# Where the squares of the first token half are taken for the MLP norm: in the tails, or where the mixers make that half

## The chip, the cores and the metric

The kernel runs on one core of a Trainium2 chip. The metric is the device time of one execution in microseconds. Engines are named as in the profile: PE does matrix products, DVE, ACT and POOL work on vectors, SP issues most of the DMAs.

## What is computed

The reference is a trunk of two layers over 1024 tokens of width 1024. Layer 0 mixes with two groups of recurrent heads, layer 1 with chunked attention. Each layer adds a mixer and then an MLP to the residual, and then a gated embedding:

```python
x = x + mix                                    # mix = heads' output @ w_out
hf = rmsnorm(x, norm_ffn_g[i])                 # x * rsqrt(mean(x*x) + eps) * g
x = x + jnp.square(jax.nn.relu(hf @ mlp_w1[i])) @ mlp_w2[i]
x = x + rmsnorm(p[i] @ ple_w_proj[i], ple_norm_g[i]) * jax.nn.sigmoid(x @ ple_w_gate[i])
```

The change is about `mean(x*x)` in the second line: one sum of 1024 squares for each token.

## The kernel before

Data stand with the 1024 features on 8 tiles of 128 partitions (n = 0..7) and the tokens along the free dimension. The tokens are worked on in two halves of 512 (`hs[0]`, `hs[1]`). Products are in float32 split into a high and a low part, so that one product of 128x128 by 128x512 is three matmuls (`mm3`): high with high, low with high, high with low. A "dense" is one output tile for one half: 8 such triples, 24 matmuls into one PSUM bank.

`trunk` runs, for each layer, the mixer with its lanes (`layer0_in`, `layer1_in`) and then `tail(i)`.

The mixer's last lane is `out_early` (L1798). It waits for the heads' results of the first half, and for n = 0..7 makes the output projection of that half as one dense; its `ev` adds the residual on DVE (L1829) and sends the sum x to DRAM as `xh[n]` (L1830, on SP). Then it makes the first part of the second half's projection (`part`): those matmuls need heads of the second half, of which the last come late in layer 0, since its recurrence runs through all tokens.

The tail begins with the second half's projection and with the norm's input. For each n:

- `load_x` (L1320, L1321) fetches the residual's second half (from `in_x` in layer 0, from `xd` in layer 1) and `xh[n]` into the buffer `xr[n % 2]`.
- `first_half` (L1339, L1340) splits the first half, scaled by the norm's weight, into high and low parts on ACT and DVE; `scaled` (L1324, ACT) keeps a scaled copy; `square(n, 0)` adds its squares to `accs[0]`.
- `ev_out` (from L1354) does the same for the second half when its dense is done: DVE adds, SP sends `xm[n]`, `scaled`, and `square(n, 1)` adds to `accs[1]`. Differences of quarters for the MLP's products (`combine` L1348, splits L1304 and L1308) come in between.
- `square` (L1331, L1334, L1335) is a Square on ACT into one of two `sq` buffers and an add into the accumulator on POOL; for n = 0 the Square goes straight into the accumulator.

The MLP multiplies blocks of weights (not of activations) by activations that aren't normalised yet; the norm's factor is put on its results. Each of its block products is cut into seven products of sums of quarters, m = 1..7 in `order`. After the fifth of them (q == 4) `row_sums` (L360) multiplies 4 + 4 pieces of the two accumulators by a column of ones on PE (`ones,acc`); after the sixth, `row_norms` scales the sums on DVE (`ms`, L374) and takes the inverse square root in 13 small steps on POOL (L274 to L279, result `col`). `to_rows` (L377) then turns `col` into rows with 8 transposes on PE (`ident,col`, L178) and two ACT copies into `rs` (L385), with which POOL scales the first results (`late<-late,rs`).

The order on each engine: the program is scheduled when it is built, by a scheduler with a model of its own, which orders an engine's instructions freely as far as their dependences allow. In the tail's MLP the products and the vector steps are pinned to the written order; the transposes of `to_rows` are not. Buffers are pools of tagged tiles: `act` gives out tiles of a pool with 6 places for the tag "a". Two PSUM banks serve the mixer's denses, 6 more the tail's.

In layer 1, `out_early` reads the residual's first half into tiles of four n (`xt`), and `acc` is the tile in which `ple_proj`, which ran ahead of it, summed squares of its own; it is free after that.

Of the kernel before, what the change touches and what calls it, by code (L numbers as in the profile page):

```python
# [8 lines left out]
F32 = mybir.dt.float32  # L9
F32R = mybir.dt.float32r  # L10
I32 = mybir.dt.int32
AF = mybir.ActivationFunctionType
ALU = mybir.AluOpType
# [4 lines left out]
P = 128  # L18
T = 1024
D = 1024  # L20
NK = D // P
HB = 512
NT = T // P
# [92 lines left out]
class Trunk:  # L116
# [252 lines left out]
    def row_norms(self, ps, out, scale=1.0 / D, eps=1e-6, pool=False):  # L369

        nc = self.nc
        nt = out.shape[-1]
        ms = self.sm.tile([P, NT], F32, tag="ms", name="ms")[:, 0:nt]
        nc.vector.tensor_scalar(ms, ps[:, 0:nt], scale, eps, op0=ALU.mult, op1=ALU.add)  # L374
        self.rsqrt_small(out, ms, [P, nt], "n", pool)

    def to_rows(self, col, out):  # L377

        nc = self.nc
        for hf in range(col.shape[-1] // 4):  # L380
            pb = self.stat_bank()
            for j in range(4):
                i = hf * 4 + j
                self.tr(pb[:, j * P:(j + 1) * P], col[:, i:i + 1].broadcast_to((P, P)), self.ident)
            nc.scalar.copy(out[:, hf * HB:(hf + 1) * HB], pb)  # L385
# [174 lines left out]
    def l0_in(self, units):  # L560
        nc, a, fr = self.nc, self.a, self.fr
        self.state = {}
        self.xg = []
        for u, (nm, p, hf) in enumerate(units):
            if u % 8 == 0:
# [3 lines left out]
                if hf == 0:  # L569
                    acc = fr.tile([P, HB], F32, tag="rsbc", name="acc", bufs=2)  # L570
# [75 lines left out]
        rsb = lambda: fr.tile([P, HB], F32, tag="rsbc", name="xs", bufs=2)  # L646
# [1 line left out]
        sc = [self.pair(q, F32) for q in (2, 3)]  # L648
        sc = [t[:, e] for t in sc for e in range(2)]
        yield from self.ple_proj(0, lambda k, hf: pt[k][:, hf], sc[0], lambda n: sc[1 + n % 3], rsb, self.load_w)  # L650
        yield from self.out_early(0, a["x"], self.pair, rsb, self.load_w, [("post", 7), ("post", 13), ("post", 14), ("post", 15)])

    def load_x(self, q, pool, tag):

# [579 lines left out]
    def tail(self, i, xsrc):  # L1234
# [9 lines left out]
        nc, tc, a = self.nc, self.tc, self.a  # L1244
# [3 lines left out]
        with ExitStack() as es:  # L1248
# [43 lines left out]
            accs = [self.accp.tile([P, HB], F32, tag=f"acc{hf}", name="acc") for hf in range(2)]  # L1292
            col = self.cst.tile([P, NT], F32, tag="col", name="col")
# [29 lines left out]
            def scaled(n, hf):  # L1323
                A.activation(xs[:, n % 2, hs[hf]], xr[n % 2][:, hs[hf]], AF.Copy, scale=self.vec("ffng", 8 * i + n))  # L1324
            b11, b12, b21, b22 = quarters(xs)

            def square(n, hf):

                t = xr[n % 2][:, hs[hf]]
                if n == 0:  # L1330
                    A.activation(accs[hf], t, AF.Square)  # L1331
                else:
                    sq = sqs()
                    A.activation(sq, t, AF.Square)  # L1334
                    G.tensor_tensor(accs[hf], accs[hf], sq, op=ALU.add)  # L1335

            def first_half(n):
                c, t, g = cmb[1 + n % 2][n // 2], xr[n % 2][:, hs[0]], self.vec("ffng", 8 * i + n)
                A.activation(c[:, 0], t, AF.Copy, scale=g)  # L1339
                V.scalar_tensor_tensor(c[:, 1], t, g, c[:, 0].bitcast(F32), op0=ALU.mult, op1=ALU.subtract)  # L1340
                scaled(n, 0)
                square(n, 0)

            def combine(m, j):
                if m == 3:
# [125 lines left out]
            def at(slot, f, *args):  # L1471
                jobs.setdefault(slot, []).append((f, *args))
# [99 lines left out]
            for q, m in enumerate(order):  # L1572
                for f, *args in ahead[q]:
                    f(*args)
                part_0[m] = product(0, m, range(4 if q < 2 else 3))
                if q < 2:
                    at(q + 2, ev_1, 0, q, m, part_0[m])
                do(q)
                if q == 4:
                    stats = self.row_sums(accs, col)  # L1580
                elif q == 5:
                    self.row_norms(stats, col, pool=True)
                yield 0
            for q, m in enumerate(order[2:]):
                for f, *args in ahead[q + 7]:
# [24 lines left out]
            x = tiles_x(F32)  # L1610
# [184 lines left out]
                nc.sync.dma_start(out=self.pnd[n], in_=t)  # L1795
        self.row_stats([acc[:, 0, :], acc[:, 1, :]], self.prsc)

    def out_early(self, i, xsrc, pair, xt, load_w, keys):  # L1798

        nc, a = self.nc, self.a  # L1800
        self.xh = [self.dr.tile([P, HB], F32, tag=f"xh{k}", name="xh") for k in range(NK)]
        pairs = [(0, 1), (2, 4), (5, 6), (3, 7)] if i == 0 else [(0, 1), (2, 3), (4, 5), (6, 7)]
        self.order = [k for pr in pairs for k in pr]

        def load(q, hf):
            raw = self.wr.tile([P, 2, HB], F32, tag="wraw", name="yr")
            t = pair(q)
            for e, k in enumerate(pairs[q]):
                y[k] = t[:, e]
                if (k, hf) == (7, 1):  # L1810
                    self.ylast = y[k]
                else:
                    nc.sync.dma_start(out=raw[:, e], in_=self.yd[k][hf])
                    self.split_scaled(y[k], raw[:, e], None, slice(0, HB))
        y, self.wod = {}, {}
        yield keys[0]
        for q in range(4):
            load(q, 0)
        for n in range(NK):
            w = load_w(a[f"w_out{i}"][n])  # L1820
            if n > 2 - i:
                self.wod[n] = self.dr.tile([P, 2, T], F32, tag=f"wod{n}", name="wod")
                for e in range(2):
                    nc.sync.dma_start(out=self.wod[n][:, e], in_=w[e].bitcast(F32))
            x = xt()
            nc.sync.dma_start(out=x, in_=xsrc[n][:, 0:HB])

            def ev(ps):
                nc.vector.tensor_tensor(x, x, ps, op=ALU.add)  # L1829
                nc.sync.dma_start(out=self.xh[n], in_=x)  # L1830
            yield from self.dense_part(w, y, ev, self.order)
        y = {}
        yield keys[1]
        ws = []
        for q in range(3):
            load(q, 1)
            if q < 2:
                ws.append(load_w(a[f"w_out{i}"][q]))
        if i == 0:
            raw = self.wr.tile([P, T], F32, tag="wraw", name="wraw")  # L1840
            nc.sync.dma_start(out=raw, in_=a["w_out0"][2])
            self.w_next = self.split_w(raw, T, [self.pre.tile([P, T], F32R, tag=f"p{q}", name="w" + q) for q in "hl"])
        self.first = [self.bank() for _ in ws]

        def part(ks):
            for (hi, lo), ps in zip(ws, self.first):
                for k in ks:
                    o = slice(k * P, k * P + P)
                    self.mm3(ps, hi[:, o], lo[:, o], y[k][:, 0, :], y[k][:, 1, :], k == 0, k == 7)
                    yield 0  # L1850
        yield from part(self.order[:6])
        yield keys[2]
        load(3, 1)
        self.mark(("ylast", 0))
        yield from part(self.order[6:7])
        yield keys[3]
        yield from part([7])
        self.y = y
# [21 lines left out]
    def attn_ins(self, steps, l1):  # L1880
        kv = {}
        for s, (pr, hf) in enumerate(steps):
            if s >= 3:
                yield ("at", s - 3)
            self.st[s] = yield from self.attn_in(pr, hf, l1, kv)
            self.mark(("qk", s), self.lat["qk"])

        act = self.act
        ws = {}

        def load_w(src):
            n = ws["n"] = ws.get("n", -1) + 1
            if n % 3 == 0:
                ws["h"], ws["l"] = self.weights3(n // 3 % 2)
            raw = self.wr.tile([P, T], F32, tag="wraw", name="wraw")
            self.nc.sync.dma_start(out=raw, in_=src)
            hi, lo = ws["h"][:, n % 3, :], ws["l"][:, n % 3, :]
            self.nc.scalar.copy(hi, raw)
            self.nc.vector.tensor_tensor(lo, raw, hi.bitcast(F32), op=ALU.subtract)
            return hi, lo  # L1900
        p = [act([P, 2, T], F32R, "b") for _ in range(2)]
        acc = act([P, 2, HB], F32)
        t = [act([P, 2, 2, HB], F32) for _ in range(4)]
        yield from self.ple_proj(1, lambda k, hf: p[k][:, :, hf * HB:hf * HB + HB], acc, lambda n: t[n // 2][:, n % 2],
                                 lambda: self.wp.tile([P, HB], F32, tag="sq", name="sq", bufs=1), load_w)
        q = {}

        def xt():
            n = q["n"] = q.get("n", -1) + 1
            if n % 4 == 0:  # L1910
                q["x"] = act([P, 4, HB], F32)
            return q["x"][:, n % 4, :]
        yield from self.out_early(1, self.xd, lambda q: act([P, 2, 2, HB], F32R), xt, load_w,
                                  [("at", 14), ("at", 14), ("at", 14), ("at", 15)])

    def attn_norms(self, steps, l1):
        K = []
# [311 lines left out]
```

## Time and profile before

| | us |
|---|---|
| median of 3 executions (lowest, highest) | 3065.73 (3061.58, 3071.53) |
| the profiled execution, on the device clock | 3063.73 |
| its span from the first to the last instruction | 3062.0 |

The mean granted clock of PE over the span is 0.975 of full speed. The stretches that the change touches, in time on the profile's clock:

| stretch | what runs there |
|---|---|
| 819 to 879 | layer 0: the 8 denses of `out_early` beside the recurrence |
| 879 to 917 | layer 0: first parts of the second half, and the recurrence's last steps |
| 917 to 957 | layer 0's tail: second half of the projection, first halves read back |
| 957 to 987 | layer 0: MLP products 1 to 7, the norm's sums and factor |
| 2247 to 2290 | layer 1: the 8 denses of `out_early` |
| 2290 to 2335 | layer 1's tail: second half of the projection |
| 2335 to 2366 | layer 1: MLP products 1 to 7, the norm's sums and factor |

A row of a timeline gives start, duration, engine, line, operation, `out<-in`, shapes, how many instructions the row joins, and in brackets how long the engine stood before it and who let it go. A row of windows gives for a stretch its length, then for each engine the busy time and the number of instructions, then PE's granted clock, the mean busy share of the DMA engines, and GB/s.

### The profile page before, as it was taken

To read this page: it belongs to the slowest core of one execution; us is meant where nothing else is said; L and a number is where in the kernel's file an instruction comes from. 1 tells how busy PE (TensorE), PEld (TensorE's weight loads), DVE (VectorE), ACT (ScalarE), POOL (GpSimd) and SP (SyncE) were. 2 spreads that over 40 slices of the span, in tenths; PEclk is the share of its full clock that TensorE was granted. 3 is DMA by queue.
4 is the path that set the end of the run, shared out by engine and by line. 5 is a ranking of instruction groups with operands and counts; after the bars stand their busy time and mean duration, and the time that the engine had idled before them with its cause. 6 is when DMAs were issued, how large, how long until landed. Compare 5 with 4: busy or idle time off the path is not lost. (4 is left out here: it accounts for less than half of the span.)

```text
span 3062.0 us, 45242 instructions
## 1 busy us (share of the span) xinstructions
PE 2958.2 (97%) x16888; PEld 2488.1 (81%) x16888; DVE 2217.9 (72%) x3680; ACT 1409.4 (46%) x2546; POOL 1255.6 (41%) x1396
## 2 busy tenths in 40 slices
PE   8999999998989999999999999999999999999999
PEld 6888778877877888788888899998887888788887
DVE  6756765667748888877676687877858888877672
ACT  4444443434435544543333466656645544543331
POOL 5535533444504666645445100000204666645442
PEclk9999989998999999999999999999999999999999
DMA  3231212212444434655323211110275444654322
GB/s 129 95 96 56 74 45 77 75 60 76 154 158 177 155 151 151 237 203 176 123 91 122 71 45 41 41 57 17 78 283 188 155 152 151 232 207 176 123 94 100
DMA packets 166765, 374.31 MB, mean 122 GB/s; under 512 B 41360, under 2 KB 45584, under 8 KB 165136
## 3 DMA queue, kind: packets, MB, share of 16 engines
q1 hardware_dynamic: 134288, 312.68, 29.6%
q10 hardware_dynamic: 32256, 58.73, 5.1%
q8 instruction: 133, 2.18, 0.3%
q14 instruction: 88, 0.72, 0.1%
HBM read 259.15 MB, written 112.20 MB: 121 GB/s over the span
## 5 line engine op out<-in xcount | busy, mean ns | idle before, releaser
L173 PE MATMUL dps<-r,act 128*128 128x512 f32 x4440 | 1043.0, 394 | 9.6 <-DVE act L113 8.3
L173 PEld LDWEIGHTS dps<-r,act 128*128 128x128 f32 x4440 | 836.2, 189 | 199.9 <-DVE act L113 16.1
L173 PE MATMUL dps<-xg,whi 128*128 128x512 f32 x1248 | 421.4, 416 | 14.6 <-ACT xg L342 7.1
L113 ACT CAST act<-late 128x512 fp32r<-128x512 f32 (+1 forms) x282 | 205.5, 731 | 445.4 <-DVE late L113 263.2
L113 DVE TENSOR_TENSOR act<-late,act 128x512 fp32r<-128x512 f32 (+1 forms) x282 | 330.9, 1175 | 71.7 <-ACT act L113 68.4
L173 PE MATMUL dps<-wq,act 128*128 128x384 f32 x1536 | 302.8, 345 | 6.9 <-DVE vs L1987 2.5
L173 PEld LDWEIGHTS dps<-xg,whi 128*128 128x128 f32 x1248 | 237.9, 196 | 65.1 <-ACT xg L342 7.1
L173 PEld LDWEIGHTS dps<-wq,act 128*128 128x128 f32 x1536 | 264.3, 190 | 12.2 <-DVE vs L1987 4.1
L173 PE MATMUL dps<-xg,wlo 128*128 128x512 f32 x624 | 257.3, 413 | 0.8 <-DVE wlo L299 0.8
L113 POOL TENSOR_TENSOR late<-late 128x512 f32<-128x512 f32 (+1 forms) x104 | 186.5, 1802 | 78.6 <-ACT late L113 57.0
L113 POOL TENSOR_TENSOR late<-late,rs 128x512 f32<-128x512 f32 x88 | 137.5, 1575 | 102.1 <-DVE late L113 94.1
L1994 POOL TENSOR_TENSOR sq<-qk 128x512 f32<-128x512 f32 x32 | 35.7, 1116 | 312.4 <-ACT qk L1982 286.9
L113 DVE TENSOR_TENSOR r<-act,r 128x1024 fp32r<-128x1024 f32 (+1 forms) x80 | 140.3, 1755 | 6.7 <-ACT r L113 6.7
L173 PEld LDWEIGHTS dps<-xg,wlo 128*128 128x128 f32 x624 | 121.7, 195 | 26.5 <-DVE wlo L299 1.2
L113 DVE TENSOR_TENSOR late<-late 128x512 f32<-128x512 f32 x120 | 142.3, 1186 | 1.0
L173 PE MATMUL dps<-xw,act 128*128 128x512 f32 x576 | 139.1, 394 | 3.1 <-ACT act L113 3.1
L173 PEld LDWEIGHTS dps<-xw,act 128*128 128x128 f32 x576 | 108.5, 189 | 27.8 <-ACT act L113 3.5
L2082 ACT ACTIVATE pb<-pb,mx 128x640 f32<-128x640 f32 (+4 forms) x128 | 89.5, 699 | 85.5 <-DVE mx L2080 83.1
L299 DVE TENSOR_TENSOR wlo<-wraw,whi 128x1024 fp32r<-128x1024 f32 x76 | 96.0, 1264 | 36.6 <-ACT whi L298 35.6
L298 ACT CAST whi<-wraw 128x1024 fp32r<-128x1024 f32 x76 | 79.5, 1048 | 89.5 <-PE dps L173 56.7
L113 DVE TENSOR_TENSOR late<-late,dps 128x512 f32<-128x512 f32 x154 | 104.7, 682 | 19.7 <-ACT late L113 15.5
L113 ACT ACTIVATE late<-late 128x512 f32<-128x512 f32 x176 | 110.6, 631 | 13.4 <-POOL late L113 9.8
(504 smaller groups left out, 5823.6 us busy)
## 6 DMA issues: line engine op xcount, KB each, us to landing
late<-in_w SPq DMA_DIRECT2D x100, 512.0 KB
hc<-late ACTq DMA_DIRECT2D x154, 256.0 KB
act<-hc SPq DMA_DIRECT2D x76, 512.0 KB
wraw<-in_w_in SPq DMA_DIRECT2D x56, 512.0 KB
hraw<-hc SPq DMA_DIRECT2D x36, 512.0 KB
hc<-sums ACTq DMA_DIRECT2D x70, 256.0 KB
act<-in_w SPq DMA_DIRECT2D x28, 512.0 KB
wraw<-in_w_out SPq DMA_DIRECT2D x21, 512.0 KB
```

Source lines behind the costliest of these rows:

```text
L113: return lambda *args, **kw: self.tc.keep_in_program_order(f(*args, **kw))
L173: r = self.nc.tensor.matmul(out, lhsT, rhs, start=start, stop=stop)
L298: nc.scalar.copy(hi, raw)
L299: nc.vector.tensor_tensor(lo, raw, hi.bitcast(F32), op=ALU.subtract)
L1994: G.tensor_tensor(sq, q4[:, 8 * e:8 * e + 8], q4[:, 8 * e:8 * e + 8], op=ALU.mult)
L2082: A.activation(S, S, AF.Exp, bias=mx[:, 1:2], accum_out=l)
```

## The change

`square(n, 0)` leaves the tail's `first_half`. In its place `out_early` takes the squares of each x of the first half while it is still on chip: an ACT Square and a POOL add for each n (for n = 0 the Square alone, into the accumulator). Behind the eighth dense it makes the 4 sums of that half on PE and scales them on DVE into columns 0 to 3 of a new tile `mlp_ms`. The tail makes only the second half's 4 sums, scales them into columns 4 to 7, and takes the inverse square root of all eight as before. In layer 0 the accumulator is a new tile (`acch`) and the squares go through the tiles of `t2`; in layer 1 the accumulator is the first half of `ple_proj`'s tile, which so stays in use longer, and the squares go through one buffer `sq` of its pool.

```diff
+    def mean_squares(self, ps, ms, scale=1.0 / D, eps=1e-6):
+
+        self.nc.vector.tensor_scalar(ms, ps[:, 0:ms.shape[-1]], scale, eps, op0=ALU.mult, op1=ALU.add)
...
                 scaled(n, 0)
-                square(n, 0)
...
                 if q == 4:
-                    stats = self.row_sums(accs, col)
+                    stats = self.row_sums(accs[1:], col[:, 4:8])
                 elif q == 5:
-                    self.row_norms(stats, col, pool=True)
+                    self.mean_squares(stats, self.mlp_ms[:, 4:8])
+                    self.rsqrt_small(col, self.mlp_ms, [P, NT], "n", True)
...
-    def out_early(self, i, xsrc, pair, xt, load_w, keys):
+    def out_early(self, i, xsrc, pair, xt, load_w, keys, acc, sqt):
...
             def ev(ps):
                 nc.vector.tensor_tensor(x, x, ps, op=ALU.add)
                 nc.sync.dma_start(out=self.xh[n], in_=x)
+                sq = sqt() if n else acc
+                nc.scalar.activation(sq, x, AF.Square)
+                if n:
+                    nc.gpsimd.tensor_tensor(acc, acc, sq, op=ALU.add)
             yield from self.dense_part(w, y, ev, self.order)
+        self.mlp_ms = self.cst.tile([P, NT], F32, tag="mlpms", name="mlpms")
+        self.mean_squares(self.row_sums([acc], self.mlp_ms[:, 0:4]), self.mlp_ms[:, 0:4])
```

(The calls pass, in layer 0, `self.l0.tile([P, HB], F32, tag="acch", name="acch")` and `self.t2`, in layer 1 `acc[:, 0]` and a tile "sq" of `self.wp` with one buffer.)

What the scheduler makes of it is seen in the engines' orders. Each engine has as many instructions as before. The first place is layer 0's MLP, from the sums on. PE before (`ones,acc` are the sums, `ident,col` the transposes of `to_rows`, all other rows the products' matmuls):

```order
L173 MATMUL dps<-ones,acc 128x1 x8
L173 MATMUL dps<-r,act 128x512 x9
L173 MATMUL dps<-act 128x512 x9
L173 MATMUL dps<-xw_10071,act 128x512 x3
L173 MATMUL dps<-x_10073,act 128x512 x3
L173 MATMUL dps<-r,act 128x512 x6
L173 MATMUL dps<-act 128x512 x3
L173 MATMUL dps<-r,act 128x512 x12
L178 MATMUL dps<-ident,col 128x128 x8
```

And PE now, at the same place:

```order
L173 MATMUL dps<-ones,acc 128x1 x4
L173 MATMUL dps<-r,act 128x512 x9
L173 MATMUL dps<-act 128x512 x9
L173 MATMUL dps<-xw_10101,act 128x512 x3
L173 MATMUL dps<-x_10103,act 128x512 x3
L173 MATMUL dps<-r,act 128x512 x6
L178 MATMUL dps<-ident,col 128x128 x4
L173 MATMUL dps<-act 128x512 x3
L173 MATMUL dps<-r,act 128x512 x12
L178 MATMUL dps<-ident,col 128x128 x4
```

The first four transposes now stand 30 matmuls behind the sums, where all eight stood 45 behind them. In the same stretch DVE's scaling of the sums moved. DVE before (`ms` is the scaling, the other rows are splits and differences of the products):

```order
L113 TENSOR_TENSOR act<-act 128x512 x2
L113 TENSOR_TENSOR xw_10071<-act,xw_10071 128x512
L374 TENSOR_SCALAR ms<-dps 128x8
L113 TENSOR_TENSOR r<-act,r 128x512
L113 TENSOR_TENSOR act<-act 128x512
L113 TENSOR_TENSOR act<-late,act 128x512
L113 TENSOR_TENSOR x_10073<-act,x_10073 128x512
```

And DVE now, where the scaling writes `mlpms` (L379):

```order
L113 TENSOR_TENSOR act<-act 128x512 x2
L113 TENSOR_TENSOR xw_10101<-act,xw_10101 128x512
L113 TENSOR_TENSOR r<-act,r 128x512
L113 TENSOR_TENSOR act<-act 128x512
L113 TENSOR_TENSOR act<-late,act 128x512
L379 TENSOR_SCALAR mlpms<-dps 128x4
L113 TENSOR_TENSOR x_10103<-act,x_10103 128x512
```

Three more operations of 128x512 stand ahead of it.

The second place is the same one in layer 1. PE now, from the sums on (before, its rows are those of layer 0 before, with all eight transposes 45 matmuls behind the sums):

```order
L173 MATMUL dps<-ones,acc 128x1 x4
L173 MATMUL dps<-r,act 128x512 x9
L173 MATMUL dps<-act 128x512 x9
L173 MATMUL dps<-xw_22298,act 128x512 x3
L173 MATMUL dps<-x_22300,act 128x512
L178 MATMUL dps<-ident,col 128x128 x4
L173 MATMUL dps<-x_22300,act 128x512 x2
L173 MATMUL dps<-r,act 128x512
L178 MATMUL dps<-ident,col 128x128 x4
```

Here the first four stand 22 matmuls behind the sums, the others three matmuls further. DVE's scaling stands one operation earlier than before, ahead of the split of `xw`.

The third place is the end of layer 1's mixer. PE now, where the first two rows are the last matmuls of the eighth dense and the last two the first ones of the second half's first part (`act` in the row of the sums is the accumulator):

```order
L173 MATMUL dps<-act,wq_22132 128x512 x2
L173 MATMUL dps<-act,wq_22133 128x512
L173 MATMUL dps<-ones,act 128x1 x4
L173 MATMUL dps<-act,wq_22132 128x512 x2
L173 MATMUL dps<-act,wq_22133 128x512
```

Before, the same matmuls follow each other without the row of the sums. In layer 0 the sums (`ones,acch`) stand further behind the eighth dense: between them are nine rows of the recurrence's small matmuls, and 20 matmuls of the second half's first part that stood among those now come after the sums.

Two smaller moves: on SP, in layer 0's tail, the load of the last `in_x` tile (n = 7) stood behind the loads of `xh[6]` and `xh[7]` and now stands ahead of both; on DVE there, the add of L1354 for n = 7 moved ahead of the last two differences of L1348 and of L1340 for n = 6. In layer 1's mixer the loads of the residual's first half for n = 4 to 7 stand behind the fourth dense's `ev`.

More of the change, by code (lines that the diff above doesn't have):

```diff
@@ L373, in row_norms @@
         ms = self.sm.tile([P, NT], F32, tag="ms", name="ms")[:, 0:nt]
-        nc.vector.tensor_scalar(ms, ps[:, 0:nt], scale, eps, op0=ALU.mult, op1=ALU.add)
+        self.mean_squares(ps, ms, scale, eps)
         self.rsqrt_small(out, ms, [P, nt], "n", pool)
+    def mean_squares(self, ps, ms, scale=1.0 / D, eps=1e-6):
+        self.nc.vector.tensor_scalar(ms, ps[:, 0:ms.shape[-1]], scale, eps, op0=ALU.mult, op1=ALU.add)
     def to_rows(self, col, out):
@@ L650, in l0_in @@
         yield from self.ple_proj(0, lambda k, hf: pt[k][:, hf], sc[0], lambda n: sc[1 + n % 3], rsb, self.load_w)
-        yield from self.out_early(0, a["x"], self.pair, rsb, self.load_w, [("post", 7), ("post", 13), ("post", 14), ("post", 15)])
+        yield from self.out_early(0, a["x"], self.pair, rsb, self.load_w, [("post", 7), ("post", 13), ("post", 14), ("post", 15)],
+                                  self.l0.tile([P, HB], F32, tag="acch", name="acch"), self.t2)
     def load_x(self, q, pool, tag):
@@ L1913, in attn_ins @@
         yield from self.out_early(1, self.xd, lambda q: act([P, 2, 2, HB], F32R), xt, load_w,
-                                  [("at", 14), ("at", 14), ("at", 14), ("at", 15)])
+                                  [("at", 14), ("at", 14), ("at", 14), ("at", 15)], acc[:, 0],
+                                  lambda: self.wp.tile([P, HB], F32, tag="sq", name="sq", bufs=1))
     def attn_norms(self, steps, l1):
```

## The prediction

> **What bounds the kernel now.** I read the page first: the span and the busy time of each engine.
>
> ```profile
> span 3062.0 us, 45242 instructions
> PE 2958.2 (97%) x16888; PEld 2488.1 (81%) x16888; DVE 2217.9 (72%) x3680; ACT 1409.4 (46%) x2546; POOL 1255.6 (41%) x1396
> ```
>
> PE is busy for 2958.2 of 3062.0 us, so all that can be gained without taking matmuls away are 3062.0 - 2958.2 = 104 us of standing still, and what a lower clock costs. The change takes no matmul away, and ACT and POOL have room everywhere on average. So the question is only which of PE's waits it removes and which it makes. I therefore read windows around the places that it touches, then the timelines of PE and of those for whom PE waits there.
>
> ```profile
> core 0: us, PE busy (x) PEld busy (x) DVE busy (x) ACT busy (x) POOL busy (x), PEclk, DMA share, GB/s
> 953.90:963.00 9.10, 3.82 (x15) 2.58 (x14) 8.35 (x11) 6.82 (x12) 5.91 (x4) 0.79 0.43 141
> 962.00:967.00 5.00, 5.00 (x14) 3.96 (x15) 5.00 (x8) 2.76 (x5) 1.06 (x1) 0.60 0.74 249
> 2255.80:2260.80 5.00, 4.97 (x21) 4.04 (x22) 2.61 (x3) 1.05 (x1) 0.00 (x0) 1.00 1.02 411
> ...
> 2344.70:2349.70 5.00, 5.00 (x15) 3.75 (x16) 4.23 (x5) 3.32 (x6) 1.29 (x1) 0.66 0.32 107
> ```
>
> The first row is the start of layer 0's tail MLP: PE works 3.82 of 9.10 us, DVE 8.35. That is the place which the change means to relieve. The rows at 962.00 and 2344.70 show what follows a stall: for 5 us the granted clock is 0.60 and 0.66, which loses 5 x 0.40 = 2.0 and 5 x 0.34 = 1.7 us more.
>
> **The sums and the norm's factor in layer 0 (a new wait).** Behind the squares comes a chain from PE over DVE and POOL back to PE. First PE, then DVE's scaling, then the first, a late and the last of POOL's 13 steps:
>
> ```profile
> 961.97 1.22 PE L173 MATMUL dps<-r,w 128*128 128x512 f32 x2 [4.06 <-DVE r L1340]
> ...
> 973.33 1.84 PE L173 MATMUL dps<-ones,acc 128*128 128x1 f32 x16
> 975.03 2.32 PE L173 MATMUL dps<-r,act 128*128 128x512 f32 x9
> ...
> 982.03 1.25 PE L173 MATMUL dps<-act 128*128 128x512 f32 x3
> ...
> 985.86 1.03 PE L178 MATMUL dps<-ident,col 128*128 128x128 f32 x8
> ```
>
> ```profile
> 975.20 0.17 DVE L374 TENSOR_SCALAR ms<-dps 128x8 f32<-128x8 f32 x1 [0.69 <-PE dps L173]
> ```
>
> ```profile
> 975.47 0.57 POOL L274 TENSOR_SCALAR col<-ms 128x8 int32<-128x8 int32 x1 [4.86 <-DVE ms L374]
> ...
> 981.25 0.20 POOL L276 TENSOR_TENSOR rsw<-col 128x8 f32<-128x8 f32 x1
> ...
> 982.63 0.52 POOL L279 TENSOR_TENSOR col<-col,rsw 128x8 f32<-128x8 f32 x1
> ```
>
> POOL's chain takes 982.63 + 0.52 - 975.47 = 7.7 us and was done at 983.15, 2.7 us before PE came to the transposes at 985.86. That slack goes. The 30 matmuls between the rows at 975.03 and 982.03 take 7.0 us, 0.233 each. The sums now take half of 975.03 - 973.33 = 1.70, so they end 0.85 earlier, near 974.2, and PE comes to the first transposes near 974.2 + 7.0 = 981.2. DVE's scaling, though, now stands behind three more operations. DVE is free at 974.5 (0.69 before 975.20), three of 0.61 from start to start bring the scaling's end to 976.5, and POOL's chain to 976.6 + 7.7 = 984.3. Stall: 984.3 - 981.2 = 3.1. From below: the POOL steps with an idle DVE beside them take 0.20 (row at 981.25) against 0.52 to 0.57, and nine such would save 3 us, so 0; from above 4, should DVE be later still. I take 3.0, since DVE is busy in this stretch. The products' matmuls are queued on PE behind the waiting transposes, and PE has no other work in this stretch, so the whole stall is on the path.
>
> For the clock after it I have stalls on both sides: 0.88 us ahead of 2255.83 was followed by 1.00 (the row at 2255.80), 3.08 ahead of 2344.69 by 0.66. A stall of 3 us costs between 0 and 1.7 more; I take 1.2. Layer 0's transposes: **+4.2**.
>
> **The sums behind layer 1's mixer (a new wait).** Rows of the eighth dense's end, and of a Square and an add of the same shapes in the tail:
>
> ```profile
> 2255.83 44.39 PE L173 MATMUL dps<-act,wq 128*128 128x512 f32 x191 [0.88 <-DVE act L1829]
> ```
>
> ```profile
> 2278.25 0.69 DVE L1829 TENSOR_TENSOR act<-act,dps 128x512 f32<-128x512 f32 x1 [3.48 <-PE dps L173]
> ...
> 2289.29 0.69 DVE L1829 TENSOR_TENSOR act<-act,dps 128x512 f32<-128x512 f32 x1 [2.25 <-PE dps L173]
> ```
>
> ```profile
> 2295.30 0.61 ACT L1331 ACTIVATE acc<-late 128x512 f32<-128x512 f32 x1
> ```
>
> ```profile
> 2298.04 1.29 POOL L1335 TENSOR_TENSOR acc<-acc,sq 128x512 f32<-128x512 f32 x1 [61.83 <-ACT sq L1334]
> ```
>
> PE runs from 2255.83 for 44 us without a gap, the eighth dense and the first parts behind it in one row. Now four sums stand right behind that dense, and they need its own result: PE to DVE 0.69, ACT 0.61, POOL 1.29, together 2.59, and four hand-overs, for which the rows at 975.20 and 975.47 show 0.10; with 0.1 to 0.2 each the wait is 3.1. Behind the sums wait the first parts' matmuls, whose operands are there: all of it is on the path. From below 2.6, from above 5, if the Square waits on ACT for other casts. With the clock as above: **+4.3**. The sums themselves (+0.85 here and in layer 0's mixer) are the ones that the tails lose: 0 in all.
>
> The loads of x for n = 4 to 7 come later in this stretch. The row at 2278.25 shows DVE waiting 3.48 for PE and not for a load; so I cost them at nothing, with 2 us from above.
>
> **Layer 0's mixer.** Its sums stand behind the recurrence's next steps, which depend on each other:
>
> ```profile
> 878.94 0.69 DVE L1829 TENSOR_TENSOR xs<-xs,dps 128x512 f32<-128x512 f32 x1 [0.77 <-PE dps L173]
> ```
>
> ```profile
> 878.71 1.05 ACT L298 CAST whi<-wraw 128x1024 fp32r<-128x1024 f32 x1 [1.35 <-PE dps L173]
> ...
> 881.95 0.36 ACT L482 COPY TZ<-iz 64x256 f32<-64x256 f32 x1
> ```
>
> The last step ahead of the sums needs the copy that ends at 882.31. The sums' own chain, from the eighth dense's add at 878.94, needs that add, a Square behind the cast that ends at 879.76, and the add: 879.76 + 0.61 + 1.29 = 881.7 and the hand-overs, about 882. PE had 20 matmuls (20 x 0.233 = 4.7 us) to do among these steps; now it does them later, where they cover the same recurrence. The steps go ahead by about as much as their cover was, so I take **+0.5**, between 0 and 2.
>
> **The starts of the tails (what is removed).** Layer 1, PE, DVE (an operation alone, then two of the same kind), POOL:
>
> ```profile
> 2344.69 2.80 PE L173 MATMUL dps<-xw,act 128*128 128x512 f32 x6 [3.08 <-ACT act L113]
> ```
>
> ```profile
> 2333.84 0.69 DVE L1308 TENSOR_TENSOR xw<-act,xw 128x512 fp32r<-128x512 f32 x1
> 2334.44 3.50 DVE L1308 TENSOR_TENSOR act<-act 128x512 fp32r<-128x512 f32 x2
> ```
>
> ```profile
> 2334.12 4.97 POOL L1335 TENSOR_TENSOR acc<-acc,sq 128x512 f32<-128x512 f32 x3 [1.92 <-ACT sq L1334]
> ```
>
> Beside three POOL adds DVE's operations take 3.50/2 = 1.75 instead of 0.69, 1.06 more each, and the ACT split for which PE then waits 3.08 stands behind them. Two of the three adds go: 2 x 1.06 = 2.1 off DVE's queue, and a Square of 0.61 off ACT's. What is left of the stall, 3.08 - 2.7 = 0.4, is too short to touch the clock (by the 0.88 above), so 1.7 of that goes as well: -2.7 - 1.7 = **-4.4**, between 0 (if something else holds that split) and -4.8.
>
> The Trainium skill, in "SBUF: two separate sides" of "SBUF — State Buffer", says that a DVE operation with two SBUF inputs and a GpSimd one that reads SBUF exclude each other for the whole instruction. By this trace's 1.75 against 0.69 it holds here. By that rule the sum is as given; without it this term would be 0.
>
> Layer 0 has the same collision, but more besides:
>
> ```profile
> 960.17 1.75 DVE L1340 SCALAR_TENSOR_TENSOR r<-act,vecs,r 128x512 fp32r<-128x512 f32 x1
> ```
>
> ```profile
> 953.27 1.96 SPq L1321 DMA_DIRECT2D act<-xh  x2
> 955.43 0.33 SPq L1320 DMA_DIRECT2D act<-in_x  x1
> ```
>
> PE waits here 4.06 for the first half of n = 6, and its load now stands behind that of 955.43 on SP, which can push it back by up to 2 us; DVE also has an add for n = 7 ahead of it. That takes back what fewer POOL adds give: **0**, between -7.3 (all 9.10 - 3.82 = 5.3 of the first window and 2.0 of clock) and +2.
>
> **The factor in layer 1.** Here DVE scales at once when the sums end: 0.17 and the hand-overs, some 0.4, and then POOL's 7.7, so that the factor is there 8.1 us behind the sums. PE comes to the transposes after 22 matmuls, 22 x 0.233 = 5.1 us behind the sums. Stall 8.1 - 5.1 = 3.0, between 0 and 4 for the reasons in layer 0, with the clock **+4.2**.
>
> **Sum.** 4.2 + 4.3 + 0.5 - 4.4 + 0 + 4.2 = +8.8. The profiled execution took 3063.73 (span 3062.0), 2.0 below the median of 3065.73. I forecast 3063.73 + 8.8 = **3072.5 us**. About 0.3%, 9 us, is what a measurement of this kernel can tell from no change: the forecast lies just inside.
>
> **Rivals.**
>
> *Relief wins.* Both starts are freed (-7.3 and -4.8) and POOL's steps run at 0.20 so that no transpose waits: -7.3 - 4.8 + 0.5 + 4.3 = -7.3, 3056.4; with the mixer's wait hidden as well, -11.6, 3052.1. For it: the collisions are plain in DVE's rows. Against it: in the MLP DVE has no gaps beside the chain, and SP's order in layer 0. Chance 0.10, of which 0.07 past 9 us.
>
> *Layer 1's start isn't relieved (slower).* If the split for which PE waits at 2344.69 comes late for its weights' load and not for DVE, the stall moves with PE and stays: +8.8 + 4.4 = +13.2, 3076.9. It decides where the relief is under 4 us: then the sum passes 9. For it: the release is ACT's, not DVE's. Against it: the two slow DVE rows stand in that split's own queue and lose 2.1 of the 3.08. Chance 0.20.
>
> *No clock cost.* A stall of 3 us that leaves the clock alone, as 0.88 did: 8.8 - 3 x 1.2 = +5.2, 3068.9. Against it: 0.66 after 3.08. Chance 0.15. The Trainium skill, "Part 1: The HAM clock gate (the "warmup" mystery)" of "TensorE: Matmul & The Clock Gate", has the clock halved after an idle window of about 3.4 us; by that rule this rival would be the likely one. The trace's drop after 3.08 speaks against taking it so strictly.
>
> *Nothing to see.* The squares pass from one idle ACT and POOL to another, and the new waits are as short as layer 0's sums: about 0 to +1, 3064. Against it: PE's order in three places. Chance 0.10.
>
> **How the numbers follow.** The forecast has 0.45. Within 0.3%: 0.15 + 0.10 of the last two rivals, 0.03 of the first, and a little over half of the forecast, 0.24: 0.52. Slower: 0.20 and the other 0.21 of the forecast: 0.41. Faster: 0.07. By the bounds the sum goes from -7.3 - 4.8 + 2.6 = -9.5 (all else 0) to +24 (4 + 1.7 at each of the transposes, 5 + 1.7 in layer 1's mixer, 2 in layer 0's, 2 at its tail's start, 2 for the loads); not all ends come together. The range 3061 to 3083 leaves out the first rival and the far end of the slow side.
>
> **What would show it.** PE rows `ident,col` with a wait of 2 to 4 us for POOL in both tails, four of them ahead of the last products; a wait of about 3 us for POOL ahead of `ones,act` near 2290; no wait for ACT's `act` near 2345, with DVE's splits at 0.69; in layer 0 still a stop of 4 to 6 us near 958 for L1345. A granted clock of 1.00 behind the new waits would show the clock terms wrong; transposes without a wait, or a stop in layer 0 that is gone, would make the whole prediction too high.

## The result, and the profile after

The changed kernel takes 3090.44 us (median of 4 executions, 3085.93 to 3096.88) beside 3065.52 for the kernel before. The ratio is 1.0089, with a 95% interval of 1.0072 to 1.0105: some 27 us slower (25 by the medians), three times what I forecast, and outside my range. Of the runs further below, one execution of d took 4767.49 us at a mean clock of 0.553; it counts in none of the ratios.

The page's span and engines, after:

```profile
span 3084.2 us, 45269 instructions
PE 2981.2 (97%) x16888; PEld 2490.1 (81%) x16888; DVE 2201.9 (71%) x3682; ACT 1411.7 (46%) x2546; POOL 1259.6 (41%) x1396
```

PE stands still for 3084.2 - 2981.2 = 103 us; before it was 104. So the waits have not grown in sum. PE's **busy** time has, by 2981.2 - 2958.2 = 23 us, for the same 16888 records of matmuls. The clock explains little of it: in the records of the granted clock PE stands at half clock for 160.8 us instead of 155.8, which loses 2.5 more. The page's costliest group says where; first before, then after (busy us, mean ns of one, idle time ahead):

```profile
L173 PE MATMUL dps<-r,act 128*128 128x512 f32 x4440 | 1043.0, 394 | 9.6 <-DVE act L113 8.3
```

```profile
L173 PE MATMUL dps<-r,act 128*128 128x512 f32 x4440 | 1059.7, 397 | 8.9 <-DVE act L113 7.6
```

The MLP's products of `r` with `act` take 16.7 us more. Windows in the middle of layer 0's MLP, far from anything that the change touches, show the same plainly. Before, then after:

```profile
1310.00:1500.00 190.00, 190.00 (x832) 156.06 (x831) 135.90 (x114) 71.88 (x75) 91.16 (x33) 1.00 0.48 162
```

```profile
1310.00:1500.00 190.00, 190.00 (x816) 152.85 (x815) 128.30 (x109) 70.04 (x74) 92.51 (x33) 1.00 0.47 156
```

In both PE is busy for all 190 us at a granted clock of 1.00. Before, it starts 832 matmuls in that time, after, 816: 2% fewer, without a wait and without a lower clock. No step of the prediction has a term for this.

The waits that I did forecast are there in part. (Two things that stand otherwise ahead of the prediction: DVE has two instructions more than before, 3682 for 3680, since the scaling of each layer is now two; and PE's order also changes in the last steps of layer 1's attention, between 2208 and 2259.) The end of layer 1's mixer, after (PE; then POOL, ACT and SP in the same stretch; then windows, with the clock in the third column from the end):

```profile
2300.09 1.87 PE L173 MATMUL dps<-ones,act 128*128 128x1 f32 x8 [5.14 <-POOL act L1839]
2301.82 14.12 PE L173 MATMUL dps<-act,wq 128*128 128x512 f32 x48
```

```profile
2298.26 1.77 POOL L1839 TENSOR_TENSOR act<-act,sq 128x512 f32<-128x512 f32 x1 [6.11 <-ACT sq L1837]
```

```profile
2296.61 1.04 ACT L1909 CAST wq<-wraw 128x1024 fp32r<-128x1024 f32 x1 [3.29 <-DMA wraw<-in_w_out]
2297.56 0.63 ACT L1837 ACTIVATE sq<-act 128x512 f32<-128x512 f32 x1
```

```profile
2276.59 2.36 SPq L1831 DMA_DIRECT2D act<-xd  x4
...
2293.33 0.33 SPq L1907 DMA_DIRECT2D wraw<-in_w_out  x1
```

```profile
2300.00:2307.60 7.60, 7.51 (x22) 6.25 (x23) 2.64 (x5) 2.29 (x5) 0.04 (x1) 0.50 0.98 338
2307.60:2320.00 12.40, 12.40 (x55) 9.98 (x54) 4.71 (x6) 5.20 (x11) 1.29 (x1) 1.00 0.80 314
```

PE waits 5.14 us for the last square's add. That Square stands on ACT behind a cast of weights, whose load came late on SP, and so it starts 1.9 us after its data (the add on DVE ended at 2295.67). Behind the wait PE runs at half clock for 7.6 us, which loses 3.8 more.

In layer 0's MLP, after (PE, then DVE's scaling and POOL's last step):

```profile
953.47 0.50 PE L173 MATMUL dps<-r,w 128*128 128x512 f32 x1 [0.31 <-ACT r L1344]
956.89 1.22 PE L173 MATMUL dps<-r,w 128*128 128x512 f32 x2 [2.92 <-DVE r L1345]
...
977.23 0.65 PE L178 MATMUL dps<-ident,col 128*128 128x128 f32 x4
```

```profile
968.20 0.68 DVE L113 TENSOR_TENSOR act<-late,act 128x512 fp32r<-128x512 f32 x1
970.16 0.16 DVE L379 TENSOR_SCALAR mlpms<-dps 128x4 f32<-128x4 f32 x1 [1.28 <-PE dps L173]
```

```profile
976.97 0.20 POOL L279 TENSOR_TENSOR col<-col,rsw 128x8 f32<-128x8 f32 x1
```

The transposes don't wait: the three operations ahead of DVE's scaling were done at 968.88, and DVE then stood 1.28 us for PE. POOL's last step ended at 977.17, 0.06 before PE came. Layer 1's MLP, PE after:

```profile
2355.05 3.60 PE L173 MATMUL dps<-xw,act 128*128 128x512 f32 x15
...
2369.74 0.65 PE L178 MATMUL dps<-ident,col 128*128 128x128 f32 x4 [2.30 <-POOL col L279]
```

The stop of 3.08 us that stood among the `xw,act` products is gone, their 15 run in one row; the transposes wait 2.30.

### The profile page after: what moved, and what is told of

Same layout as the page of the kernel before. It is cut to its first block, busy times and chain, and to the rows that moved or that the text cites. A ratio compares the mean times of both kernels' runs of the same rounds, so it can differ in the third digit from the quotient of the medians.

```text
span 3084.2 us, 45269 instructions
## 1 busy us (share of the span) xinstructions
PE 2981.2 (97%) x16888; PEld 2490.1 (81%) x16888; DVE 2201.9 (71%) x3682; ACT 1411.7 (46%) x2546; POOL 1259.6 (41%) x1396
## 5 line engine op out<-in xcount | busy, mean ns | idle before, releaser
L173 PE MATMUL dps<-r,act 128*128 128x512 f32 x4440 | 1059.7, 397 | 8.9 <-DVE act L113 7.6
L173 PEld LDWEIGHTS dps<-r,act 128*128 128x128 f32 x4440 | 836.3, 189 | 214.6 <-DVE act L113 10.1
```

Source lines behind the costliest of these rows:

```text
L173: r = self.nc.tensor.matmul(out, lhsT, rhs, start=start, stop=stop)
```

## The experiments

All comparisons are with the kernel before on the same chip (its median was 3065.88 in the first four, 3065.43 in the next, 3063.42 in the last). Differences "by the medians" between two changed kernels can be of kernels measured beside different series of the kernel before; the ratios differ from them by up to some 3 us. An "address" is a tile's place in bytes within a partition. In a product, the 128x128 operand is called the weights, the 128x512 one the moving tile; in a row `dps<-r,act`, `r` is the moving tile and `act` the weights.

| kernel | median us | ratio to before (95%) |
|---|---|---|
| a: before, 32 unused bytes | 3081.57 | 1.0050 (1.0030 to 1.0069) |
| b: before, 64 unused bytes | 3077.84 | 1.0034 (1.0022 to 1.0046) |
| c: changed, 64 bytes for 32 | 3086.43 | 1.0071 (1.0049 to 1.0094) |
| d: c with late sums | 3083.76 | 1.0054 (1.0033 to 1.0075) |
| e: before, 192 unused bytes | 3054.58 | 0.9975 (0.9964 to 0.9987) |
| f: changed, 160 unused bytes on the right | 3067.30 | 1.0008 (0.9999 to 1.0018) |
| g: f with late sums | 3063.23 | 0.9992 (0.9982 to 1.0002) |
| h: g with pinned transposes | 3050.16 | 0.9958 (0.9946 to 0.9970) |
| i: h with 224 bytes on the right | 3059.91 | 0.9990 (0.9977 to 1.0002) |
| j: f with its own accumulator | 3066.70 | 1.0004 (0.9994 to 1.0015) |
| k: f with pinned transposes | 3064.26 | 0.9997 (0.9984 to 1.0009) |
| l: h with its own accumulator | 3046.21 | 0.9937 (0.9925 to 0.9949) |

### Are the products slower because of addresses? (a, b, c)

What products of `r` and `act` have in common, and the two groups named next have not, is that one tile lies on the left side of the memory and one on the right. The new tile of sums takes 32 bytes among the constants on the left, and all left tiles allocated behind it move by 32; the right ones stay. In the built programs the first `r` lies at 2848 before and at 2880 after; the first `act` at 163808 in both. In the trace, products of two right tiles (`xw,act`) or two left ones (`r,gw`) kept their rate or nearly so (229.3 and 228.8 ns from start to start, 226.8 and 226.9). So I gave the old kernel such a tile, unused:

```diff
             yield from self.dense_part(w, y, ev, self.order)
+        self.cst.tile([P, NT], F32, tag="pad", name="pad")
```

> The kernel before with one unused tile of 32 bytes per partition among the constants, where the change has its new tile of sums; every instruction and its order are as before, only the tiles allocated behind it (those that the products read as r and late among them) lie 32 bytes further. Theory 'address': in the trace of the change a product of r and act starts every 233.3 ns and before every 228.9, while products whose two tiles both moved or both stayed kept theirs; so this kernel shows 233.3 as well and is 14 to 20 us slower than before (4440 matmuls by 4.4 ns is 19.5; the busy time of that group grew by 16.7). Rival 'company': the products are slower because of what runs beside them in the changed order; then this kernel is as before, 0 +- 5 us, at 228.9.

It is 15.3 us slower (0.0050 of 3065.88). Its window:

```profile
1310.00:1500.00 190.00, 190.00 (x816) 152.86 (x815) 130.55 (x109) 69.96 (x73) 91.09 (x33) 1.00 0.47 155
```

816 matmuls, as in the changed kernel, with no instruction of it changed in kind or order. The address alone does it; the rival "company" falls.

For b the tile has `2 * NT` columns, for c the changed kernel's own tile has:

```diff
-        self.mlp_ms = self.cst.tile([P, NT], F32, tag="mlpms", name="mlpms")
+        self.mlp_ms = self.cst.tile([P, 2 * NT], F32, tag="mlpms", name="mlpms")[:, 0:NT]
```

> The same with an unused tile of 64 bytes. Theory 'address', in the form that the places modulo 64 bytes decide: as before, 0 +- 5 us, r with act every 228.9 ns. Should any move of the one set of tiles against the other cost, it is as slow as with 32 bytes. Rival 'company': 0 +- 5 us.

> The changed kernel with its new tile of sums given 64 bytes instead of 32, of which 32 stay unused; order as changed. Theory 'address': r with act every 228.9 ns again, 14 to 20 us faster than the changed kernel, that is 5 to 11 us slower than before, for the wait and the low clock behind layer 1's mixer. Rival 'company': 25 us slower than before, as the changed kernel.

Both miss. With 64 bytes the old kernel is still 10 us slower (820 matmuls in the window), and c is not 14 to 20 us faster than the changed kernel but 4 by the medians, 5.5 by the ratios, whose intervals overlap. My first form of the theory, that the places modulo 64 decide, falls: there is no return at 64.

### Late sums at these addresses (d)

```diff
-        self.mean_squares(self.row_sums([acc], self.mlp_ms[:, 0:4]), self.mlp_ms[:, 0:4])
         y = {}
...
         yield from part(self.order[:6])
+        self.mean_squares(self.row_sums([acc], self.mlp_ms[:, 0:4]), self.mlp_ms[:, 0:4])
```

> The kernel with 64 bytes, and with the first half's sums written behind the first six products of the second half's first parts instead of right behind the eighth dense; on PE they then stand, in layer 1, behind all the first parts. Theory 'wait': the 5.14 us that PE waited for the last square's add, and the about 4 us that the half clock behind it cost, go: 9 us faster than the kernel with 64 bytes alone, 4 us faster to 2 us slower than before. Rival: the second half's first parts meet a wait of their own (their loads come behind the same queue), and no more than 3 us are gained.

The wait at the sums is gone, as PE shows:

```profile
2302.05 8.18 PE L173 MATMUL dps<-act,wq 128*128 128x512 f32 x34 [1.19 <-ACT act L339]
2310.40 1.02 PE L173 MATMUL dps<-ones,act 128*128 128x1 f32 x8 [0.17 <-DVE late L1358]
```

But only 2.7 us are gained by the medians, not 9, and the two intervals overlap. That was nearer to the rival; but the wait for the first parts' cast that it names gives back only 1.19. The edit also gave PE another order at two far places: in layer 1's attention (1955 to 2135), and in layer 0's MLP, where the first four transposes now come so early that they wait, as in the changed kernel they did not:

```profile
976.36 0.65 PE L178 MATMUL dps<-ident,col 128*128 128x128 f32 x4 [2.42 <-POOL col L279]
```

So d is not a test of the wait at the sums alone.

### Which distance is the good one? (e, f)

With six traces I sorted all products of 128x128 by 128x512 by the distance from the weights' address to the moving tile's, and took the mean time from one start to the next. For `r` with `act` it is 2848 - 163808 = -160960 before, which is 64 modulo 256. Modulo 256 sorts them; so I put all at 0: in e with an unused tile of `6 * NT` columns (192 bytes) in the old kernel, in f with an unused pool ahead of the right side's:

```diff
+                ctx.enter_context(t.pool("padr", side="right")).tile([P, 40], F32, tag="padr", name="padr")
                 t.actA = ctx.enter_context(t.pool("actA", side="right"))
```

> The kernel before with an unused tile of 192 bytes at the same place as in the first two kernels; order as before. Over all traces so far, products of 128x128 by 128x512 sort by one number: the distance in bytes between the moving tile and the weights, modulo 256. At 0 they start every 226.7 to 228.5 ns, at 64 every 229.1 (r with act in the kernel before), at 96 every 233.5 (the changed kernel), at 128 every 232.9, at 160 and 192 every 234.2 and 233.3. Here all are at 0. Theory 'distance modulo 256': 226.7 for r with act, 4740 products by 2.2 ns, 9 to 12 us faster than before. Rival: the kernel before has the best place and any move costs; then 10 to 16 us slower, as with 32 and 64 bytes.

> The changed kernel, its order untouched, with an unused tile of 160 bytes ahead of the tiles of the right side, so that all distances are 0 modulo 256 here too. Theory 'distance': 4733 products go from 233.5 to between 226.7 and 228.5, 24 to 32 us faster than the changed kernel, 0 to 8 us faster than before; and against the kernel with 192 bytes it shows what the change costs by itself at equal addresses: 4 to 10 us slower than that. Rival 'company': within 5 us of the changed kernel.

The windows of e and f:

```profile
1310.00:1500.00 190.00, 190.00 (x840) 157.41 (x840) 136.03 (x114) 73.38 (x77) 91.74 (x33) 1.00 0.50 165
```

```profile
1310.00:1500.00 190.00, 190.00 (x840) 157.43 (x839) 137.53 (x115) 73.09 (x76) 91.90 (x33) 1.00 0.50 165
```

840 in both, more than ever. e is 10.8 us faster than before by the medians, inside the 9 to 12 expected, and 7.7 by the ratio (interval 4 to 11): the kernel before did not have the best place either. f is 23.1 faster than the changed kernel by the medians, a little under the 24 to 32 expected, and 24.8 by the ratios, with PE's instructions in the changed order. It was also expected to be 0 to 8 faster than before, and is 1.9 slower, within what can't be told from no change.

All traces together, products of `r` with `act` (about 4350 in each), at full clock and without those that a wait follows:

| distance modulo 256 | kernels | mean ns from start to start |
|---|---|---|
| 0 | e, f, g, h, j, k, l | 226.9 to 227.0 |
| 64 | before, i | 229.2, 229.2 |
| 96 | changed, a | 233.6, 233.6 |
| 128 | b, c, d | 232.8 to 233.1 |

At equal distances the change itself costs 0.0033 of 3065 (f less e): 10.1 us, or 12.7 by the medians. The expectation was 4 to 10.

### The change's own waits, at distance 0 (g, h, j, k, l)

g is f with the late sums of d. h pins the transposes:

```diff
-        return self.nc.tensor.transpose(out, in_, ident)
+        r = self.nc.tensor.transpose(out, in_, ident)
+        return self.tc.keep_in_program_order(r) if self.pinned else r
```

> That kernel with the first half's sums written behind the first six products of the first parts, as before with 64 bytes. Theory 'wait': the wait of 5.1 to 5.3 us goes and 1.2 of another comes, as in the pair with 64 bytes, where 2.7 us were gained: 2 to 5 us faster than with the sums right behind the dense. Rival: 0 +- 2, since the last square is late for its own reason and something else waits.

> That kernel with the transposes of the norm's factor pinned to the written order, in which they stand 45 products behind the sums as before the change. Theory 'wait': the 2.3 to 2.5 us that PE waits for POOL's factor in layer 1 go: 2 to 3 us faster than the kernel without the pin. Rival: 0 +- 2, if the scaled results are then late and PE waits for those, or a reordering elsewhere eats it.

g gains 4.1 us, as expected (the intervals of f and g just overlap). h gains 13.1 where 2 to 3 were expected. It isn't the one wait that was expected to go. In g, as in d, layer 0's transposes wait too:

```profile
974.78 0.65 PE L178 MATMUL dps<-ident,col 128*128 128x128 f32 x4 [2.42 <-POOL col L279]
```

The pin takes away this wait and the one of 2.44 in layer 1. And h has another order in layer 1's attention than g: from 1948 to 2126 it is again that of before, which g had left, and in the last steps (2199 to 2253) one of its own. So I pinned the transposes in f (k), where nothing else moves but them:

> The changed kernel at distance 0, with only the transposes of the norm's factor pinned to the written order; on PE nothing else moves. Theory 'wait': the 2.46 us in layer 1 go, in layer 0 there was no wait: 2 to 3 us faster than without the pin. Rival: what depends on the scaled results waits instead, 0 +- 2. The 13 us that the pin brought together with the late sums had an other order of layer 1's attention in them, which this kernel doesn't have; so neither theory expects them here.

PE at layer 1's transposes, in f (first row) and in k, where they have no wait:

```profile
2359.70 0.65 PE L178 MATMUL dps<-ident,col 128*128 128x128 f32 x4 [2.46 <-POOL col L279]
```

```profile
2362.52 2.93 PE L173 MATMUL dps<-r,act 128*128 128x512 f32 x12
2365.29 1.34 PE L178 MATMUL dps<-ident,col 128*128 128x128 f32 x8
```

3.0 us by the medians, as expected; the intervals of f and k overlap, the wait of 2.46 in f's trace is gone in k's. Where h gains on g can be read by matching PE's rows in the two traces one by one, one execution of each (h shorter by 15.9): 3.1 us around layer 0's transposes, 3.7 from the start of layer 1's MLP to its transposes, and 6.4 in the last steps of layer 1's attention (2182 to 2242 in g). No run has the order of those last steps alone, so that part stays argued.

j gives layer 1 its own accumulator in f, l in h:

```diff
-                                  [("at", 14), ("at", 14), ("at", 14), ("at", 15)], acc[:, 0],
+                                  [("at", 14), ("at", 14), ("at", 14), ("at", 15)], self.wp.tile([P, HB], F32, tag="acch", name="acch", bufs=1),
```

> The changed kernel at distance 0 (160 bytes), with a tile of its own for layer 1's first accumulator instead of the one that ple_proj used, so that the loads of x for n = 4 to 7 find a free place. Theory 'queue': the wait of 5.5 us at the sums is 3.1 of chain (add, square, add, hand-overs) and about 2 of a cast whose weights' load stood on SP behind those loads; so the wait falls to 3 to 4 us, and with less half clock behind it the kernel is 2 to 5 us faster than with the shared tile. Rival 'chain': the wait stays at 5 to 6, 0 +- 2.

> Late sums, pinned transposes, distance 0 and the tile of its own together. Theory 'queue': with the sums late nothing waits for them, so the tile of its own gives only the 1.4 us that PE waits for ACT's cast of the first parts: 0 to 2 us faster than without it, 15 to 17 us faster than before. Rival: the scheduler's other order in layer 1's attention costs some of the 13 us that came with the pin: up to 10 us slower.

PE at the sums, in f and in j:

```profile
2291.42 1.86 PE L173 MATMUL dps<-ones,act 128*128 128x1 f32 x8 [5.49 <-POOL act L1839]
```

```profile
2285.99 1.86 PE L173 MATMUL dps<-ones,acch 128*128 128x1 f32 x8 [3.71 <-POOL acch L1839]
```

The wait falls from 5.49 to 3.71: the queue behind the x loads was 1.8 of it, the chain 3.7. But the time hardly falls (0.6 by the medians, where 2 to 5 were expected). The edit has also given j the order of g in layer 1's attention, so it isn't a test of the tile alone, and PE waits at other places of layer 1's tail:

```profile
2318.34 16.64 PE L173 MATMUL dps<-act,late 128*128 128x512 f32 x72 [0.78 <-DMA late<-wod]
2338.97 2.56 PE L173 MATMUL dps<-r,act 128*128 128x512 f32 x10 [0.82 <-DVE act L1313]
2344.45 1.92 PE L173 MATMUL dps<-xw,act 128*128 128x512 f32 x6 [0.87 <-ACT act L113]
```

l is the fastest kernel of all: 3046.21 us, 0.9937 of before (0.9925 to 0.9949), 19 us faster (17.2 by the medians). It gains 4.0 on h by the medians where 0 to 2 were expected; the intervals overlap, and the order differs again in layer 1, so why isn't settled. The fair opponent of l is e, the old kernel at the same distance 0 (0.9975): there the change, put well, gains 8 us by the medians and 12 by the ratios, whose intervals lie apart.

### The good order at the old distance (i)

i is h with 56 columns instead of 40 in the pool on the right, which brings `r` and `act` back to 64 modulo 256.

> The kernel with late sums and pinned transposes, order untouched, with 224 unused bytes instead of 160 ahead of the right side, so that r with act is 64 modulo 256 apart as in the kernel before. It shows the change, put well, at the addresses of before. Theory 'distance': r with act every 228.9 to 229.6 ns and 9 to 12 us slower than at 0, so 3 to 6 us faster than before. Rival: the gain of that kernel is the order's alone; then it stays at 13 to 17 us faster.

It is 9.8 us slower than h, as expected, and its window has the 832 matmuls of before:

```profile
1310.00:1500.00 190.00, 190.00 (x832) 155.91 (x831) 134.43 (x111) 73.29 (x78) 91.61 (x33) 1.00 0.48 158
```

PE's order is the same in h and i, so the address costs much the same in the good order (9.8) as in the old one (10.8 between before and e, by the medians). At the distance of before, the change put well is 3.5 us faster by the medians, within what can't be told from no change.

## Why the prediction was wrong

**The step that failed** is in its first part: "So the question is only which of PE's waits it removes and which it makes." That took a product's duration as given. The new tile of 32 bytes moved it: PE's busy time grew by 23 us, and of the 27 us, 15.3 are had by adding such a tile to the old kernel (a). No term and no rival had it. The order, on which I spent all my rows, can't show it: a's order is that of before.

The steps that I did have sum to +8.8; at equal distances the change costs 10 to 13 (f against e). So the part about waits was nearly right in sum, but by luck: its terms were wrong in both directions. Matching PE's rows in e's and f's traces one by one (one execution of each, f longer by 10.4 in all; ahead of the change's first place the two already lie up to 3 us apart) gives +3.1 in layer 0's mixer, -1.4 in layer 0's tail, +10.3 in layer 1's mixer, -7.5 at the start of layer 1's tail, and +5.2 from its transposes on. The forecast had +0.5, +4.2, +4.3, -4.4 and +4.2. In the changed kernel's own trace:

- **Layer 0's transposes (+4.2)**: no wait in the changed kernel. The three operations ahead of DVE's scaling had their operands early enough to run before PE came to the sums (done 968.88, sums from 969.17, scaling 970.16). I had let them start where DVE's idle time before began. POOL's chain also took 970.42 to 977.17, 6.75 instead of 7.7, since four of its steps took 0.20 each instead of two: two beside an idle DVE, two beside DVE's `late<-late,dps`. I named that only as a lower bound.
- **Layer 1's mixer (+4.3)**: right mechanism, too small. The wait is 5.14 and its clock costs 3.8, 8.9 in all. The chain is 3.7 (j) where I had 3.1; 1.8 is the cast ahead of the Square, from the loads that I "cost at nothing" because DVE had not waited for them. They stood in SP's queue ahead of the weights' load, and that was waited for; with a tile of its own (j) that load is issued before 2274, and the cast no longer stands ahead of the last Square.
- **Layer 1's start (-4.4)**: right; the stop and its clock are gone, 4.8 us.
- **Layer 0's start (0)**: 2.92 + 0.31 = 3.2 us of waiting are left of 5.3, a gain of 2 within its bounds; the half clock around it stays as long as before (6.8 us).
- **Layer 1's transposes (+4.2)**: the wait is 2.30, not 3.0, and no lower clock followed.
- **Layer 0's mixer (+0.5)**: one wait of 0.15 us, as small as forecast. But behind it PE runs at half clock for 3.4 us (from 877), which loses 1.7, and the forecast had no clock term here. The five kernels with the sums right behind the eighth dense (changed, c, f, j, k) all have this stretch, and no other has it.
- **The clock (1.2 behind each new wait)**: 3.8 behind 5.14, none behind 2.30. One price for all was wrong: it comes in steps, and a wait's length alone doesn't say how many (below).

The rivals erred the same way: each moved waits about, none let the work itself become slower.

## What to carry to other kernels

Before costing a change's waits, look at what it allocates: a tile of 32 bytes in a pool that lives all through the program moves every tile behind it, and where PE is the bound, 2% on its products can be more than all that the change does to the waits; here 15 us against 10. In a trace after, compare how many matmuls start in a window in which PE is fully busy at full clock, before and after; a change in that number is no wait and is not found among waits. When two versions are compared for their order, give them equal addresses first; here that made a loss of 27 us into one of 10, and showed a version that beats the old kernel at its best place. When an edit moves one instruction, compare each engine's whole order, not only the place of the edit: two of the runs here (d, g) lost 2.4 us at a wait far from it.

## What the runs showed of the hardware

**The distance between the weights' and the moving tile's address sets the rate of matmuls.** By 840, 832, 820 and 816 matmuls in 190 us at full clock, for distances of 0, 64, 128 and 96 modulo 256 (moving tile less weights). The distance 0 was reached from the left (e) and from the right (f), 64 by two placements as well (before, i), so it is the distance and not one address. That the period is 256 is a fit to the values tried; 128 is excluded, since 0 and 128 differ. The sign counts: in products of `act` with `late` in layer 1's mixer the moving tile is the right one, so that they stand at 192, 160, 128 and 0 in before, a, b and e, and took 233.3, 234.3, 232.3 and 226.7 ns; so 192 isn't as good as 64. It is not the whole law: `xw` with `act`, at 0 in all kernels, took 226.6 to 229.3 ns in layer 0's tail, depending on where the left tiles lay. The cause behind it was not tried for.

**Half clock comes in pieces of 3.41 us.** In all records of the granted clock the stretches at 0.50 are 3.4, 6.8, 10.2 us and so on, up to 17.1, but for the one at a trace's end. 10.2 stand around the wait of 5.14, 6.8 around 3.71 (j), 3.4 around 2.46 (f), none around 2.30 in the changed kernel; in d, 3.4 follow the wait of 2.42 in layer 1 and none the equal one in layer 0. Length alone doesn't set it: 6.8 stand around 5.34 in c, and the wait of 3.3 to 3.5 at the end of layer 0's recurrence has 3.4 in h and 13.7 in i, which have one order. The Trainium skill, in "Part 1: The HAM clock gate (the "warmup" mystery)" of "TensorE: Matmul & The Clock Gate", gives the gate a free-running window of 3413 ns; the lengths agree with this. The stretches also make profiles of one order differ: before and a have the same order, yet 155.8 and 146.5 us at half clock.
